# A four-layer encoder trunk on one core: the first layer's sums of squares taken from x as it is loaded, two tiles of x copied by VectorE, and a new table of order shifts

## The chip, the cores and the metric

The kernel runs on one core of one Trainium2 chip. The metric is the device time of one execution in microseconds. Three runs of the kernel before took 1061.21 to 1062.21 us, with a median of 1061.58 us.

## The reference, cut to what matters

The input x is 512 frames of 1024 channels in float32. Four layers follow each other; each is one token mixer behind an RMS norm, added to x. The mixers are differential attention (layers 0 and 3 of the program, the "first" and the "last" here), a conformer convolution (layer 1, the second) and latent attention (layer 2, the third). All are causal by chunks of 64 frames.

```python
def _rms_norm(x, g):
    xf = x.astype(jnp.float32)
    y = xf * lax.rsqrt(jnp.mean(xf * xf, axis=-1, keepdims=True) + NORM_EPS)
    return (y * g.astype(jnp.float32)).astype(x.dtype)

for i in range(DEPTH):                      # DEPTH = 4
    kind, j = i % N_MIXERS, i // N_MIXERS   # N_MIXERS = 3
    if kind == 0:
        h = _rms_norm(x, a_norm_g[j])
        x = x + _diff_attention(h, a_w_in[j], ...)   # q, k, v, gate = split(h @ w_in); 8 heads
    elif kind == 1:
        h = _rms_norm(x, b_norm_g[j])
        x = x + _conformer_conv(h, b_w_in[j], ...)   # GLU, depthwise conv of 31 taps, layer norm, gate
    else:
        h = _rms_norm(x, c_norm_g[j])
        x = x + _mla(h, c_w_in[j], ...)              # low-rank q and kv, 8 heads, gate
return x
```

What the change rewrites is the mean of x*x over the channels of each frame, for the first layer alone. What it computes stays the same.

## The kernel before, in words

Everything stays in the core's memory. `X` holds x with channels on partitions, as 8 blocks of 128 channels by 512 frames. `Hh` and `Hl` hold g*x, split into a rounded high part and the low rest. Each weight is split in the same way after its load: ScalarE casts the high half, and VectorE or GpSimd subtracts to get the low half (line 519 or 522). Each product is then three matmuls, high x high, high x low and low x high (`mm3`, line 465 for each matmul). The norm's factor 1/rms is not applied to g*x but afterwards, per frame: `rs` is 1/rms and `rs2` its square, both 128 frames by 4 tiles. The evacuation of V, the gate and the norms of q and k read them.

`start` brings x in: four tiles of 128 frames by 1024 channels, in two buffers `L0_x0` and `L0_x1` of two tiles each. TensorE transposes 4 blocks of 128x128 into one PSUM buffer `L0_tr<tile><first block>`. From it ScalarE makes four blocks of `Hh` (line 495) and one 128x512 copy into `X` (line 502), and VectorE makes four blocks of `Hl` (line 531). Then `norm_block` lets ScalarE square the 8 channel blocks of `X`, each 128x512, and GpSimd add them into `L0_sqs` (7 additions, line 522). `norm_end` sums `L0_sqs` over partitions with four matmuls against a vector of ones (`L0_ss`), VectorE scales and adds the epsilon (line 540), GpSimd raises to the power -0.5 (`L0_r_y`, line 745) and VectorE writes `rs` and `rs2`.

While this goes on, the first weights are q and k's (`L0_qk0_w0`, `_w2`, `_w4`, `_w6`, two blocks of K each). Four accumulators `L0_qk0_a0` to `_a3`, one for each tile, collect them in PSUM, and V (`L0_v0_a0` to `_a3`) and the gate (`L0_g0`) follow through the same four PSUM buffers. So V's third and fourth accumulators can begin only when VectorE and ScalarE have read those of q and k.

In the second layer the last three channel blocks are convolved on TensorE: VectorE builds the matrices `L1_wa<block>_<group>` (line 519, 128x1152), TensorE multiplies them with the shifted input `L1_u4<block>` into `L1_c<block>`, and VectorE moves the result into `V` and takes its statistics. The gate blocks `L1_g1_a0` to `_a3` are scaled into `G` by VectorE with the table `L1_tab`. VectorE also builds the third layer's rope table `L2_tab` here.

In the third layer each head has four score blocks `L2_h<head>j<block>_sc`; softmax runs on VectorE and ScalarE and leaves the weights `_p`, TensorE transposes them (`_wtr`), ScalarE copies them out (`_wt`), and TensorE multiplies them with `V` into `L2_o<head>`. The output projection of the layer, `L2_o00` to `L2_o13`, starts while the last heads still run.

All engines run their own list of instructions in order. A planner in the kernel, `Plan.order`, makes these lists before anything runs: it takes nodes one by one, with its own costs for each instruction and for each buffer's release, and among the ready ones of an engine it prefers the one with the lowest priority number. That number is the place in the program plus a shift from the table `SHIFT` (line 210), which has an entry for most sections of the program on each engine:

```python
n.prio += SHIFT.get(section(n), 0)
```

## Time and profile before

| what | value |
|---|---|
| median of three runs | 1061.58 us (1061.21 to 1062.21) |
| the profiled execution | 1064.24 us, span 1062.4 us |
| TensorE busy | 1010.8 us, 95% |
| VectorE busy | 764.4 us, 72% |
| ScalarE busy | 586.1 us, 55% |
| GpSimd busy | 216.0 us, 20% |
| bytes moved by DMA | 87.53 MB |
| clock granted to TensorE, mean | 0.987 |

The profiled execution is one run; it is 2.66 us above the median, and all durations below come from it. An engine's busy time is the time in which it executes instructions, so the 5% that TensorE lacks are gaps in its list. In the timelines a row gives the start and the length in us, the engine, the line, the operation, what it writes and reads, how many instructions the row holds, and in brackets how long the engine idled before it and which instruction ended that wait. Buffer and layer numbers are left out of the names there.

### The profile page before, as it was taken

What the parts mean: (1) busy time and instruction counts of PE and PEld (TensorE: products, weight loads), DVE (VectorE), ACT (ScalarE), POOL (GpSimd) and SP (SyncE); (2) the same over time, 40 slices, a digit from 0 to 9 for tenths busy, and PEclk for the clock granted to TensorE, in tenths of its full rate; (3) what the DMA queues carried; (4) which work ended last, traced back from release to release, by engine and by line L of the source; (5) the groups of instructions that cost most, each with busy time, mean ns of one, the idle gap of its engine ahead of it and who ended that gap; (6) DMA issues with size and microseconds to landing.
All of it is one profiled execution on the core that took longest, in us unless ns stands there. A gap on an engine that the chain in (4) does not pass through costs nothing.

```text
span 1062.4 us, 15183 instructions
## 1 busy us (share of the span) xinstructions
PE 1010.8 (95%) x5212; PEld 847.7 (80%) x5212; DVE 764.4 (72%) x1966; ACT 586.1 (55%) x1226; POOL 216.0 (20%) x142
## 2 busy tenths in 40 slices
PE   8899999998999999798999999999999999999798
PEld 6688788887887887687887778788878888887687
DVE  4767689795669998768344769964683699989651
ACT  6557266657644556653343667753443746666642
POOL 3500000000012899960530001000210000000000
PEclk9999999998999999999999999999999999999899
DMA  7252241314014332220222211112232514423102
GB/s 240 83 138 61 80 119 60 100 48 117 31 51 128 110 104 87 79 91 1 58 91 65 85 50 60 41 38 80 80 100 85 153 41 119 112 68 101 39 20 80
DMA packets 74309, 87.53 MB, mean 82 GB/s; under 512 B 17110, under 2 KB 47702, under 8 KB 74233
## 3 DMA queue, kind: packets, MB, share of 16 engines
q1 hardware_dynamic: 74232, 86.57, 27.5%
q8 instruction: 41, 0.67, 0.3%
q14 instruction: 36, 0.29, 0.1%
HBM read 75.28 MB, written 2.10 MB: 73 GB/s over the span
## 4 chain that ended last, share of the span: by engine, by line
PE 70%; POOL 8%; ACT 8%; DVE 5%; issue 4%; DMA 2%; SPq 2%; DVEq 0%; ACTq 0%; POOLq 0%
PE L_o L465 21%; PE L_qk_a L465 15%; PE L_g_a L465 10%; PE L_v_a L465 7%; PE L_ab_a L465 5%; POOL L_cq L522 4%; POOL L_sqs L522 2%; ACT G L495 1%; SPq L569 1%; PE L_c_a L465 1%; PE L_qk_tr L471 1%; PE L_h7j_sc L465 1%; PE L_h2j_sc L465 1%; PE L_h6j_sc L465 1%; DMA L_setup<-a_lam_k 1%
## 5 line engine op out<-in xcount | busy, mean ns | idle before, releaser
L465 PE MATMUL L_qk_a<-L_qk_w,Hh 128*128 128x512 f32 x512 | 163.1, 400 | 2.6 <-DVE L_qk_T L519 1.3
L465 PE MATMUL L_o<-L_y,L_o_w 128*128 128x512 f32 x576 | 143.3, 398 | 0.3 <-DVE L_y L531 0.2
L465 PEld LDWEIGHTS L_o<-L_y,L_o_w 128*128 128x128 f32 x576 | 105.7, 189 | 21.9 <-DVE L_y L519 0.9
L465 PE MATMUL L_g_a<-L_g_w,Hh 128*128 128x512 f32 x384 | 120.8, 396 | 1.2 <-DVE L_g_w L519 0.5
L745 POOL TENSOR_TENSOR L_h_or_y<-L_h_ov,minus_half 128x4 f32<-128x4 f32 x16 | 17.5, 1093 | 465.9 <-DVE L_h_ov L540 302.3
L465 PEld LDWEIGHTS L_qk_a<-L_qk_w,Hh 128*128 128x128 f32 x512 | 91.9, 189 | 19.6 <-DVE L_qk_T L519 1.5
L465 PE MATMUL L_qk_a<-L_qk_w,Hl 128*128 128x512 f32 x256 | 100.6, 393 | 2.0 <-DVE Hl L531 2.0
L522 POOL TENSOR_TENSOR L_cq<-L_cq,L_ct 128x512 f32<-128x512 f32 x58 | 84.9, 1463 | 24.7 <-ACT L_ct L495 20.7
L465 PE MATMUL L_v_a<-L_v_w,Hh 128*128 128x512 f32 x256 | 82.5, 404 | 2.1 <-DVE L_qk_T L519 2.1
L465 PEld LDWEIGHTS L_g_a<-L_g_w,Hh 128*128 128x128 f32 x384 | 70.2, 188 | 15.9 <-DVE L_g_w L519 0.9
L465 PE MATMUL L_ab_a<-Hh,L_ab_w 128*128 128x512 f32 x256 | 80.1, 391 | 0.0
L465 PE MATMUL L_g_a<-L_g_w,Hl 128*128 128x512 f32 x192 | 75.2, 391 | 0.0
L522 POOL TENSOR_TENSOR L_sqs<-L_sqs,L_sq 128x512 f32<-128x512 f32 x28 | 45.4, 1620 | 130.5 <-ACT L_sq L495 129.1
L531 DVE SCALAR_TENSOR_TENSOR L_c<-L_u,L_tab,L_c 128x512 f32<-128x512 f32 x90 | 65.6, 749 | 1.5
L519 DVE TENSOR_TENSOR L_g_w<-L_g_w_r,L_g_w 128x1024 fp32r<-128x1024 f32 x32 | 43.5, 1360 | 28.9 <-ACT L_g_w L502 28.8
L495 ACT ACTIVATE L_ct<-L_u,L_tab 128x512 f32<-128x512 f32 x60 | 43.0, 722 | 35.1 <-POOL L_cq L522 35.0
L465 PEld LDWEIGHTS L_qk_a<-L_qk_w,Hl 128*128 128x128 f32 x256 | 48.1, 188 | 13.6 <-DVE Hl L531 3.3
L502 ACT CAST L_g_w<-L_g_w_r 128x1024 fp32r<-128x1024 f32 x32 | 33.6, 1050 | 41.7 <-PE L_v_a L465 22.0
L465 PEld LDWEIGHTS L_ab_a<-Hh,L_ab_w 128*128 128x128 f32 x256 | 48.1, 188 | 10.1
L465 PEld LDWEIGHTS L_v_a<-L_v_w,Hh 128*128 128x128 f32 x256 | 46.8, 192 | 11.6 <-DVE L_qk_T L519 2.6
L502 ACT CAST L_qk_w<-L_qk_w_r 128x1024 fp32r<-128x1024 f32 (+1 forms) x33 | 33.7, 1037 | 36.3 <-PE L_o L465 14.6
L465 PE MATMUL L_v_a<-L_v_w,Hl 128*128 128x512 f32 x128 | 50.9, 398 | 0.0
(366 smaller groups left out, 2335.6 us busy)
## 6 DMA issues: line engine op xcount, KB each, us to landing
L_qk_w_r<-a_w_in SPq DMA_DIRECT2D x62, 256.0 KB, 3.0
L_v_w_r<-a_w_in SPq DMA_DIRECT2D x16, 512.0 KB, 3.8
L_g_w_r<-a_w_in SPq DMA_DIRECT2D x16, 512.0 KB, 3.7
...
```

The lines of the kernel that those rows point to most:

```text
L465: lambda nc: nc.tensor.matmul(out.real(), a.real(), b.real(), start=start, stop=stop),
L471: emit = lambda nc: nc.tensor.transpose(out.real(), src.real(), ident.real())
L495: nc.scalar.activation(out.real(), src.real(), func, scale=scale.real() if isinstance(scale, View) else scale, **kw)
L502: lambda nc: nc.scalar.copy(out.real(), src.real()), [src], [out])
L519: lambda nc: nc.vector.tensor_tensor(out=out.real(), in0=a.real(), in1=b.real(), op=op), [a, b], [out])
L522: lambda nc: nc.gpsimd.tensor_tensor(out=out.real(), in0=a.real(), in1=b.real(), op=op), [a, b], [out])
L531: self.add("dve", out.n / 960.0 + (0.13 if isinstance(scalar, View) else 0.068), lambda nc: nc.vector.scalar_tensor_tensor(out=out.real(), ...
L569: self.add("sp", 0.45, lambda nc: nc.sync.dma_start(out.real(), src.real()), [src], [out], dma=out.n * 4 * parts)
L745: self.p.add("pool", 0.32 + 0.18 * v.n, lambda nc: nc.gpsimd.tensor_tensor(out=y.real(), in0=v.real(), in1=self.minus_half[:, 0:v.n].real( ...
```

## The change

Three things are changed. First, the copies of x's tiles 2 and 3 into `X` are made by VectorE; those of tiles 0 and 1 stay on ScalarE. Second, the first layer's sums of squares are taken from the x tiles as loaded, with frames on partitions: ScalarE squares a whole tile, 128x1024, and accumulates along the row into one column of `L0_v`; the squares themselves go to `G`, which nothing reads then. VectorE scales and adds the epsilon, and a new function `norm_root` does what the end of `norm_end` did. The 8 squares of 128x512, the 7 additions on GpSimd, the four matmuls with ones and the buffer `L0_sqs` are gone from the first layer; the other layers keep them. Third, every entry of `SHIFT` is another number (920 entries before, 884 now), so the order changes in all four layers.

```diff
 SHIFT = {k: int(v) for k, v in (x.split("=") for x in """
-L0_g0_a.act=-797 L0_g0_a.pe=27679 L0_g0_w.act=699 L0_g0_w.dve=421 L0_g0_w_r.sp=4 L0_g1_a.act=686 L0_g1_a.pe=-1737
...
+L0_g0_a.act=-41 L0_g0_a.pe=26653 L0_g0_w.act=-16 L0_g0_w.dve=1363 L0_g0_w_r.sp=-471 L0_g1_a.act=2674 L0_g1_a.pe=9
...
@@ start
-                p.copy(self.X[:, k:k + 4, ts_], tr[:, :, :])
+                p.copy(self.X[:, k:k + 4, ts_], tr[:, :, :], "act" if t < 2 else "dve")
                 for q in range(4):
                     p.stt(self.Hl[:, k + q, ts_], tr[:, q, :], self.g[:, k + q:k + q + 1],
                           self.Hh[:, k + q, ts_].f32(), ALU.mult, ALU.subtract)
-        p.shift = 150
-        for k in range(NK):
-            self.norm_block(k, split=False)
-        self.norm_end()
-        p.shift = 0
+        v = self.small(4, "L0_v")
+        for t in range(NT):
+            p.act(self.G[:, t, :], tiles[t // 2][:, t % 2, :], AF.Square, accum=v[:, t:t + 1])
+        p.ts(v, v, 1.0 / D, ALU.mult, EPS, ALU.add)
+        self.norm_root(v)
@@ norm_begin
-        self.sqs = self.buf("wt", name + "_sqs", [P, S])
+        if name != "L0":
+            self.sqs = self.buf("wt", name + "_sqs", [P, S])
@@ norm_end
         v = self.small(4, N + "_v")
         p.ts(v, ps[:, :, 0], 1.0 / D, ALU.mult, EPS, ALU.add)
-        r = self.rsqrt(v, N + "_r")
+        self.norm_root(v)
+
+    def norm_root(self, v):
+        p = self.p
+        r = self.rsqrt(v, self.nname + "_r")
         p.copy(self.rs, r, "dve")
         p.tt(self.rs2, r, r, ALU.mult)
```

The lists of instructions differ in many places. Three of them follow. A row gives the line, the operation, what it writes and reads with the program's names, the shape, and how many such instructions stand together; the numbers behind the names only tell buffers apart, and all lines of the changed kernel are 5 smaller.

The first place is the start, on ScalarE and on GpSimd. ScalarE from its first instruction, before the change:

```order
L495 ACT_TABLE_LOAD
L495 ACTIVATE Hh_115<-L0_tr00_156,L0_lay_126 128x128 x4
L502 COPY X_111<-L0_tr00_156 128x4x128
L495 ACTIVATE Hh_115<-L0_tr04_162,L0_lay_126 128x128
L502 CAST L0_qk0_w0_186<-L0_qk0_w0_r_142 128x512
L495 ACTIVATE Hh_115<-L0_tr14_180,L0_lay_126 128x128 x4
L502 COPY X_111<-L0_tr14_180 128x4x128
L495 ACTIVATE Hh_115<-L0_tr10_195,L0_lay_126 128x128 x4
L502 COPY X_111<-L0_tr10_195 128x4x128
```

And with the change (`L0_lay` holds the norm's gain, `L0_qk0_w0_r` is the weight as loaded, `G`,`L0_v` are the dump and the sums of the Squares):

```order
L490 ACT_TABLE_LOAD
L490 ACTIVATE G_118,L0_v_153<-L0_x0_126 128x1024
L490 ACTIVATE Hh_115<-L0_tr04_155,L0_lay_139 128x128 x3
L497 CAST L0_qk0_w0_179<-L0_qk0_w0_r_141 128x512 x2
L490 ACTIVATE Hh_115<-L0_tr00_174,L0_lay_139 128x128 x4
L490 ACTIVATE G_118,L0_v_153<-L0_x0_126 128x1024
L490 ACTIVATE Hh_115<-L0_tr10_191,L0_lay_139 128x128 x2
L497 CAST L0_qk0_w2_213<-L0_qk0_w2_r_147 128x1024
```

A Square of the first tile now stands ahead of all blocks of `Hh`, and the second one ahead of tile 1's; the copies into `X` moved behind the casts.

GpSimd at the same place, its first work on data, with the change:

```order
L517 TENSOR_TENSOR L0_qk0_w2_213<-L0_qk0_w2_r_147,L0_qk0_w2_213 128x1024
L517 TENSOR_TENSOR L0_qk0_w4_226<-L0_qk0_w4_r_150,L0_qk0_w4_226 128x1024
L740 TENSOR_TENSOR L0_r_y_279<-L0_v_153,minus_half_114 128x4
L517 TENSOR_TENSOR L0_qk0_w6_276<-L0_qk0_w6_r_198,L0_qk0_w6_276 128x1024
L740 TENSOR_TENSOR L0_h0_or_y_916<-L0_h0_ov_911,minus_half_114 128x4
```

Before, the three low halves of `_w2`, `_w4` and `_w6` stood together, with the seven additions into `L0_sqs` and then `L0_r_y` behind them; now `L0_r_y` stands ahead of `_w6`.

The second place is VectorE in the second layer's tail, before the change:

```order
L519 TENSOR_TENSOR G_118<-L1_g1_a3_4405,L1_tab_2552 128x512
L519 TENSOR_TENSOR L1_wa5_2_4480<-L1_d4_3321,wx_112 128x1152
L519 TENSOR_TENSOR L1_wa5_3_4498<-L1_d4_3321,wx_112 128x1152
L519 TENSOR_TENSOR L1_wa6_0_4515<-L1_d4_3321,wx_112 128x1152
L519 TENSOR_TENSOR L2_tab_4521<-L2_setup_4057 128x4x64
L519 TENSOR_TENSOR L2_tab_4521<-L2_setup_4057 128x4x32
L519 TENSOR_TENSOR L1_wa6_1_4534<-L1_d4_3321,wx_112 128x1152
L519 TENSOR_TENSOR V_117<-L1_c5_4182,cb_113 128x128 x2
```

And with the change:

```order
L514 TENSOR_TENSOR G_118<-L1_g1_a2_4330,L1_tab_2528 128x512
L514 TENSOR_TENSOR L1_wa5_2_4406<-L1_d4_3297,wx_112 128x1152
L514 TENSOR_TENSOR L1_wa5_3_4425<-L1_d4_3297,wx_112 128x1152
L514 TENSOR_TENSOR L1_wa6_0_4442<-L1_d4_3297,wx_112 128x1152
L514 TENSOR_TENSOR L1_wa6_1_4454<-L1_d4_3297,wx_112 128x1152
L514 TENSOR_TENSOR V_117<-L1_c5_4085,cb_113 128x128 x4
L547 BN_STATS L1_stat_4016<-V_117 128x6 x4
L547 BN_STATS L1_stat_4016<-L1_ctr3_4449 128x6 x4
L514 TENSOR_TENSOR G_118<-L1_g1_a3_4457,L1_tab_2528 128x512
L514 TENSOR_TENSOR L2_tab_4519<-L2_setup_4026 128x4x64
```

The weight `L1_wa6_1` moved ahead of the rope table, and the last gate block, `L1_g1_a3`, behind the groups of block 5; on TensorE the four `L1_c5` groups now stand ahead of that gate block as well.

The third place is TensorE in the third layer around heads 5 and 6, before the change, from the last rows of the output projection ahead of head 5's product with `V`:

```order
L465 MATMUL L2_o03_6803<-L2_y0_6676,L2_o0_w0_6524 128x512 x6
L465 MATMUL L2_o03_6803<-L2_y1_6738,L2_o0_w2_6553 128x512 x6
L465 MATMUL L2_o01_6745<-L2_y1_6738,L2_o0_w2_6553 128x512 x6
L471 MATMUL L2_h5j0_wtr_6827<-ident_109,L2_h5j0_p_6616 128x128
L471 MATMUL L2_h5j1_wtr_6830<-ident_109,L2_h5j1_p_6637 128x128 x2
L465 MATMUL L2_h6j0_sc_6835<-L2_p3_st0_6659 128x256 x3
...
L465 MATMUL L2_o5_6853<-V_117,L2_h5j0_wt_6828 128x128
```

And with the change:

```order
L460 MATMUL L2_o00_6699<-L2_y0_6666,L2_o0_w0_6501 128x512 x3
L466 MATMUL L2_ytr3_6708<-ident_109,V_117 128x128 x4
L460 MATMUL L2_o01_6716<-L2_y0_6666,L2_o0_w0_6501 128x512 x3
L466 MATMUL L2_h5j0_wtr_6724<-ident_109,L2_h5j0_p_6577 128x128
L466 MATMUL L2_h5j1_wtr_6726<-ident_109,L2_h5j1_p_6588 128x128 x2
L460 MATMUL L2_o02_6733<-L2_y0_6666,L2_o0_w0_6501 128x512 x3
L466 MATMUL L2_p3_tr00_6741<-ident_109,L2_q3_T_6329 128x128 x4
L466 MATMUL L2_p3_tr10_6748<-ident_109,L2_q3_T_6329 128x128 x4
L460 MATMUL L2_o5_6756<-V_117,L2_h5j0_wt_6723 128x128
```

Of the output projection, 39 matmuls of 512 columns stood ahead of the first `L2_o5` row before, and 9 stand there now; head 6's scores moved behind it.

More of the change, by code (lines that the diff above doesn't have):

```diff
@@ L350 @@
-L3_v1_w.act=2427 L3_v1_w.dve=-13 L3_v1_w_r.sp=7813 L3_y0.act=-1042 L3_y1.act=4284 L3_y1.dve=-50 L3_y2.act=-30
-L3_y2.dve=-1702 L3_y3.dve=-20 L3_ytr0.pe=244 L3_ytr1.pe=-8 L3_ytr2.pe=5413 L3_ytr3.pe=1767 L3_ytr5.pe=-3471
-L3_ytr6.pe=234 L3_ytr7.pe=-11 none.act=578 none.dve=18020 none.sp=-2444
+L0_g0_a.act=-41 L0_g0_a.pe=26653 L0_g0_w.act=-16 L0_g0_w.dve=1363 L0_g0_w_r.sp=-471 L0_g1_a.act=2674 L0_g1_a.pe=9
+L0_g1_w.act=97 L0_g1_w.dve=17790 L0_g1_w_r.sp=2029 L0_h0_mx.dve=-2270 L0_h0_or_y.dve=1539 L0_h0_or_y.pool=-368
@@ new lines @@
+L1_sq3.act=-2124 L1_sq4.act=590 L1_sq5.act=-1989 L1_sq6.act=-197 L1_sq7.act=330 L1_sqs.act=1509 L1_sqs.pool=-1106
+L1_ss.pe=-9618 L1_stat.dve=1535 L1_tab.act=1801 L1_tab.dve=-152 L1_u0.dve=-2015 L1_u1.dve=1 L1_u2.dve=33073
+L1_u3.dve=-1192 L1_u45.dve=-2495 L1_u46.dve=3 L1_u46.sp=3511 L1_u47.dve=-256 L1_u47.sp=-2378 L1_v.dve=-1332
+L1_vtr.pe=2912 L1_wa5_.dve=41 L1_wa6_.dve=-1417 L1_wa7_.dve=546 L1_wxt.act=2847 L1_wxt.pe=16 L1_y0.act=250
+L1_y0.dve=5627 L1_y1.act=47 L1_y1.dve=-1188 L1_y2.act=1283 L1_y2.dve=-1229 L1_y3.act=76 L1_ytr1.pe=713
@@ new lines @@
+L2_h1_wtr.pe=-3577 L2_h2_mx.dve=-1829 L2_h2_sc.dve=380 L2_h2_sc.pe=260 L2_h2_wt.act=1436 L2_h2_wtr.pe=12579
+L2_h3_mx.dve=-1997 L2_h3_p.act=191 L2_h3_sc.dve=686 L2_h3_sc.pe=17196 L2_h3_wt.act=-241 L2_h3_wtr.pe=23947
+L2_h4_mx.dve=1 L2_h4_p.act=-1571 L2_h4_sc.dve=23559 L2_h4_sc.pe=87 L2_h4_wt.act=-1816 L2_h4_wtr.pe=1211
+L2_h5_mx.dve=-944 L2_h5_p.act=-15 L2_h5_sc.dve=1911 L2_h5_sc.pe=1205 L2_h5_wt.act=18 L2_h5_wtr.pe=1331
+L2_h6_mx.dve=1029 L2_h6_p.act=-161 L2_h6_sc.dve=-4071 L2_h6_sc.pe=-681 L2_h6_wt.act=1169 L2_h6_wtr.pe=-5297
@@ new lines @@
+L3_h1_oss.dve=-462 L3_h1_ov.dve=6 L3_h1_p.act=4811 L3_h1_p.dve=97 L3_h1_sc.dve=22663 L3_h1_sc.pe=-2103
+L3_h1_wt.act=316 L3_h1_wtr.pe=-1575 L3_h2_cf.dve=-19071 L3_h2_mx.dve=-2004 L3_h2_or_y.dve=529 L3_h2_or_y.pool=2572
+L3_h2_osq.act=-2776 L3_h2_oss.dve=-1251 L3_h2_ov.dve=-208 L3_h2_p.act=-5058 L3_h2_p.dve=38 L3_h2_sc.dve=2398
+L3_h2_sc.pe=-7821 L3_h2_wt.act=14301 L3_h2_wtr.pe=-3318 L3_h3_cf.dve=32 L3_h3_mx.dve=563 L3_h3_or_y.dve=2098
+L3_h3_or_y.pool=-116 L3_h3_osq.act=5652 L3_h3_oss.dve=-139 L3_h3_ov.dve=337 L3_h3_p.act=-370 L3_h3_p.dve=-148
@@ new lines @@
+L3_o12.pe=-7163 L3_o130.pe=-1724 L3_o131.pe=84245 L3_o1_w.act=-10417 L3_o1_w.dve=-459 L3_o1_w_r.sp=1930
+L3_o2.dve=-9008 L3_o2.pe=-3288 L3_o3.dve=2429 L3_o3.pe=-848 L3_o4.dve=-1820 L3_o4.pe=-1577 L3_o5.pe=-1710
+L3_o6.dve=1005 L3_o6.pe=-44 L3_o7.dve=-97 L3_o7.pe=-5 L3_ot000.act=-1631 L3_ot000.sp=-474 L3_ot010.sp=8
+L3_ot020.act=1104 L3_ot020.sp=1041 L3_ot030.act=-2656 L3_ot030.sp=2301 L3_ot100.act=1693 L3_ot100.sp=122
+L3_ot110.act=610 L3_ot110.sp=-420 L3_ot120.act=-2179 L3_ot120.sp=-216 L3_ot130.act=20621 L3_ot130.sp=-439
@@ new lines @@
+L3_ot13256.sp=30 L3_qk0_T.dve=577 L3_qk0_a.pe=-477 L3_qk0_ss.dve=43410 L3_qk0_st.act=-385 L3_qk0_st.dve=-1022
+L3_qk0_st.sp=1201 L3_qk0_t.dve=-19 L3_qk0_tr.pe=15880 L3_qk0_w.act=1952 L3_qk0_w.dve=4596 L3_qk0_w_r.sp=-578
+L3_qk0_y.dve=-1432 L3_qk1_T.dve=-66 L3_qk1_a.pe=47647 L3_qk1_ss.dve=171 L3_qk1_st.act=1192 L3_qk1_st.dve=-9004
+L3_qk1_st.sp=4764 L3_qk1_t.dve=-229 L3_qk1_tr.pe=-2412 L3_qk1_v.dve=22 L3_qk1_w.act=-133 L3_qk1_w.dve=976
+L3_qk1_w_r.sp=-13540 L3_qk1_y.dve=-985 L3_qk2_T.dve=-4 L3_qk2_a.pe=246 L3_qk2_sq.act=3743 L3_qk2_ss.dve=69611
@@ new lines @@
+L3_sq4.act=245 L3_sq5.act=-272 L3_sq6.act=-425 L3_sq7.act=32 L3_sqs.act=2425 L3_sqs.pool=-2404 L3_tab.dve=15
+L3_v.dve=2050 L3_v0_a.act=2798 L3_v0_a.pe=1620 L3_v0_w.act=721 L3_v0_w.dve=705 L3_v0_w_r.sp=-556 L3_v1_a.act=3413
+L3_v1_a.pe=1 L3_v1_w.act=1026 L3_v1_w.dve=5611 L3_v1_w_r.sp=1964 L3_y0.act=-14 L3_y0.dve=181 L3_y1.act=1615
+L3_y1.dve=5 L3_y2.act=303 L3_y3.act=227 L3_ytr0.pe=-146 L3_ytr1.pe=5627 L3_ytr2.pe=10596 L3_ytr3.pe=54
+L3_ytr4.pe=-1549 L3_ytr5.pe=-15504 L3_ytr7.pe=1143 none.dve=22412 none.sp=-7301
```

243 lines of the change are left out of this document (105 added, 138 removed).

## The prediction

> **What bounds the kernel now.** I read the page first, then the chain of waits, TensorE's waits by cause, and the timelines of the places where the order differs.
>
> ```profile
> span 1062.4 us, 15183 instructions
> PE 1010.8 (95%) x5212; PEld 847.7 (80%) x5212; DVE 764.4 (72%) x1966; ACT 586.1 (55%) x1226; POOL 216.0 (20%) x142
> PE 70%; POOL 8%; ACT 8%; DVE 5%; issue 4%; DMA 2%; SPq 2%; DVEq 0%; ACTq 0%; POOLq 0%
> ```
>
> ```profile
> 52.09 13.28 PE L_v_a L465 x51
> ...
> 859.86 5.48 PE L_qk_a L465 x24
> ```
>
> TensorE is busy for 1010.8 of 1062.4 us, and the change takes almost no matmul away: only its 51.6 us without work, and stretches in which it works below full speed, can be gained. The two last rows are pieces of the chain (start, length, what): V's product ends at 65.37, and the second is my unit, since 24 matmuls of 512 columns in 5.48 us are 0.228 us each, and a three-product group is 0.68 us. The waits, summed by cause, show where the idle time lies (us in total, times, the longest):
>
> ```profile
> PE L_o L465 <- DVE V L531: 6.6, 2, 3.6
> PE L_ytr L471 <- DVE V L540: 4.7, 1, 4.7
> PE L_g_a L465 <- DVE G L519: 4.4, 3, 3.0
> ...
> PE L_ss L465 <- POOL L_sqs L522: 1.7, 3, 1.0
> ```
>
> They are many and small, these four 17.4 us together, and most hang on VectorE. Only the last one, in the first of its three places, belongs to what the change rewrites by hand; the rest can move only through the new order.
>
> **The start: what is removed.** The first layer's rms statistics are made from X, the copy behind the transposes, so they come late (the timeline; in brackets how long the engine idled before, and for whom):
>
> ```profile
> 35.66 3.63 POOL L522 TENSOR_TENSOR L_sqs<-L_sqs,L_sq 128x512 f32<-128x512 f32 x1 [11.90 <-ACT L_sq L495]
> 41.97 9.01 POOL L522 TENSOR_TENSOR L_sqs<-L_sqs,L_sq 128x512 f32<-128x512 f32 x5 [0.65 <-ACT L_sq L495]
> 47.01 0.72 PE L465 MATMUL L_v_a<-L_v_w,Hh 128*128 128x512 f32 x2 [2.14 <-DVE L_qk_T L519]
> ...
> 51.03 1.05 PE L465 MATMUL L_ss<-ones,L_sqs 128*128 128x1 f32 x8 [0.96 <-POOL L_sqs L522]
> 51.95 0.84 PE L465 MATMUL L_v_a<-L_v_w,Hh 128*128 128x512 f32 x2
> ...
> 55.58 0.71 PE L465 MATMUL L_v_a<-L_v_w,Hh 128*128 128x512 f32 x2
> ```
>
> TensorE first waits 2.14 us for two accumulators that VectorE empties, then 0.96 us for GpSimd's last addition, then sums over partitions from 51.03 to 51.95, which is 0.92 us. From 51.95 to 55.58 nine matmuls take 3.63 us, 0.40 each instead of 0.228: 9 x 0.228 = 2.05, so 1.58 us are lost after the two waits. The window row of these 20 us shows the clock at 0.91:
>
> ```profile
> 40.00:60.00 20.00, 16.90 (x71) 13.25 (x70) 15.60 (x33) 6.59 (x10) 11.93 (x7) 0.91 0.35 104
> ```
>
> [...] If these waits were not its cause, the 1.58 us would stay and the sum below would lead to 1058.0; I go by the row, in which nothing else stands ahead of the slow matmuls.
>
> With the sums gone, 0.96 + 0.92 + 1.58 = 3.46 us go. The 2.14 us shrink as well, because VectorE and GpSimd hold each other up:
>
> ```profile
> 36.33 0.68 DVE L519 TENSOR_TENSOR L_qk_T<-L_qk_T,L_qk_t 128x512 f32<-128x512 f32 x1
> 42.33 1.79 DVE L519 TENSOR_TENSOR L_qk_T<-L_qk_T,L_qk_t 128x512 f32<-128x512 f32 x1
> ```
>
> At 36.33 the addition takes 0.68 us, and it is GpSimd's addition beside it that is long (3.63 us, against 9.01 for the next five). At 42.33, beside those five, the same addition takes 1.79: 1.11 more, ahead of the evacuation that TensorE waits for. I take 1.11; the bounds are 0 (what else stands before the accumulators of tiles 2 and 3 fills the gap: in the new order VectorE has four X copies and the second half of its rope products there) and 2.14 (the wait goes). Removed: 3.46 + 1.11 = **4.57 us**.
>
> **The start: what is added.** The timeline again, with the nearest rows to each new instruction:
>
> ```profile
> 19.86 1.05 ACT L502 CAST L_qk_w<-L_qk_w_r 128x1024 fp32r<-128x1024 f32 x1 [0.36 <-DMA L_qk_w_r<-a_w_in]
> 956.12 0.20 ACT L495 ACTIVATION_READ_ACCUMULATOR L_h5j_p<-L_h5j_sc,L_h5j_mx,L_rq 128x1 f32 x1
> 21.57 0.59 ACT L502 COPY X<-L_tr 128x512 f32<-128x512 f32 x1
> 33.48 0.63 ACT L495 ACTIVATE L_sqs<-X 128x512 f32<-128x512 f32 x1
> 29.18 1.44 DVE L519 TENSOR_TENSOR L_qk_t<-L_qk_a,L_tab 128x256 f32<-128x256 f32 x4 [6.11 <-ACT L_qk_sq L495]
> 20.98 2.78 POOL L522 TENSOR_TENSOR L_qk_w<-L_qk_w_r,L_qk_w 128x1024 fp32r<-128x1024 f32 x1 [3.23 <-ACT L_qk_w L502]
> 37.23 0.62 PE L465 MATMUL L_v_a<-L_v_w,Hh 128*128 128x512 f32 x2
> 52.37 1.95 POOL L745 TENSOR_TENSOR L_r_y<-L_v,minus_half 128x4 f32<-128x4 f32 x1 [1.38 <-DVE L_v L540]
> ```
>
> No row is a Square of 1024 elements. A 1024-element cast on the same engine is 1.05 us and reading an accumulator 0.20: **1.25 us** each, an estimate from these rows. Four make 5.0 us, as much as the eight old Squares (8 x 0.63 = 5.04), and four X copies (2.36) leave ScalarE. What counts is the place: the old ones begin at 33.48, and the new ones stand in the first 20 us, between the Hh blocks and weight casts that TensorE waits for. The first stands ahead of every Hh block, so I charge one in full, 1.25 us. The others stand where TensorE has groups at hand: tiles 0 and 1 now run over all of K first, 16 groups of 0.68 = 10.9 us, before tiles 2 and 3 begin. Bounds: 0 (the first Square fits into the wait for g and the weights) and 5.0 (none is covered).
>
> GpSimd's r_y now stands between the second and the last low half of the first weights. It is 1.95 us, so with nothing else changed the last low half ends at 20.98 + 2.78 + 1.95 = 25.7. Behind it 20 groups remain, 13.7 us, and one set of transposes, 0.5 as an estimate, so V would begin at 39.9, which is 2.7 later than 37.23: 1.5 more than the 1.25 charged. Against this, that weight's load now moves ahead of the setup loads on SP's queue. If the 3.23 us that GpSimd idles before it go with that, the low half ends at 22.5 and V begins at 36.7, 0.5 early. I keep the 1.25, which lies between these ends.
>
> The four X copies on VectorE have no row; its nearest PSUM operation of that size is a share of the 0.68 us row, so 2.7 us for four, against 0 if only the copied bytes counted. They lie in the 6.11 us that VectorE idles before 29.18. If the setup loads come late, they fall behind its wait for these, and the Hl blocks after them are late; that cost is within the 5.0. Start in sum: 4.57 - 1.25 = **3.32 us** gained.
>
> **The second layer's tail.** VectorE builds the next layer's rope table and a convolution weight in an order that TensorE waits for:
>
> ```profile
> 466.40 3.24 DVE L519 TENSOR_TENSOR L_tab<-L_setup 128x256 f32<-128x256 f32 x2
> 469.56 1.34 DVE L519 TENSOR_TENSOR L_wa<-L_d,wx 128x1152 f32<-128x1152 f32 x1
> 470.96 11.95 PE L465 MATMUL L_c<-L_wa,L_u 128*128 128x128 f32 x90 [1.85 <-DVE L_wa L519]
> ```
>
> 3.24 us of table stand ahead of the weight, and TensorE idles 1.85. In the new order four weights stand ahead of the table: the 1.85 go. What is late next is the gate block that now follows the convolution groups; bounds 0 and 1.85.
>
> Sum: 3.32 + 1.85 = 5.2 us. The profiled execution took 1064.24 us (its span and 1.84 around it), 2.66 above the median of the runs, 1061.58. From 1064.24 the sum leads to 1059.0; on the runs' scale **1056.4 us**. The rest of the new order I take as 0 with no view to price it: it touches rows of TensorE in all four layers, so I allow a quarter of the 17.4 us of waits above, 4 us, both ways.
>
> **Rivals.**
>
> *The lead is lost again: no change.* Further on VectorE is nearly full:
>
> ```profile
> 220.00:240.00 20.00, 20.00 (x98) 16.68 (x97) 19.47 (x49) 11.92 (x18) 0.00 (x0) 1.00 0.14 46
> ```
>
> VectorE (the third busy column) is busy 19.47 of 20 us. If it sets the pace of the first attention, TensorE arrives 3.32 us earlier and waits longer there. Against it: TensorE is busy for all 20.00 in the same row, so both are full and VectorE gains the lead too. Only the 1.85 would stay, and less if the gate block takes it: 1059.7 to 1061.6, say 1060.5. Chance 0.20.
>
> *A larger gain.* The gate blocks of the second layer are TensorE's other series of waits:
>
> ```profile
> 404.07 0.47 PE L465 MATMUL L_g_a<-Hh,L_g_w 128*128 128x512 f32 x1 [1.36 <-DVE L_ab_v L519]
> 432.50 0.47 PE L465 MATMUL L_g_a<-Hh,L_g_w 128*128 128x512 f32 x1 [3.00 <-DVE G L519]
> 439.99 0.50 PE L465 MATMUL L_g_a<-Hh,L_g_w 128*128 128x512 f32 x1 [1.65 <-DVE L_u L558]
> 446.80 0.50 PE L465 MATMUL L_g_a<-Hh,L_g_w 128*128 128x512 f32 x1 [1.05 <-DVE G L519]
> ```
>
> The new order puts the last gate block behind convolution groups. If all four go, 1.36 + 3.00 + 1.65 + 1.05 = 7.06 us more: 1056.4 - 7.1 = 1049.3. For it: the groups now ahead of the last block are free of G. Against it: the first three blocks keep VectorE's scaling ahead of them. Chance 0.16.
>
> *Slower: the third layer's heads lose their cover.* Before the first product of head 5's weights with V, TensorE now has 39 output-projection matmuls; in the new order 9 stand there. The first row here is 18 of the 39; the second is from the last layer, where heads run without such cover:
>
> ```profile
> 703.25 4.37 PE L465 MATMUL L_o<-L_y,L_o_w 128*128 128x512 f32 x18
> 986.48 0.94 PE L465 MATMUL L_o<-V,L_h5j_wt 128*128 128x128 f32 x6 [3.55 <-DVE V L531]
> ```
>
> The 30 that leave are 30 x 0.228 = 6.8 us. If softmax on VectorE and ScalarE is not ready, that much idling appears at head 5, of which the last layer shows 3.55 us in one wait. Added to the forecast, 6.8 gives 1063.2; with a slow stretch like the 1.58 behind it and the 1.5 of the late last weight it reaches 1066.3. It decides from 7.3 us of new idling on, since 5.2 + 2.1 must be used up. Against it: the 30 matmuls cover the later heads instead, and the page's waits show no idling at head 5 now, so there is some slack. Chance 0.17.
>
> **How the numbers follow.** Forecast 0.47, no change 0.20, larger gain 0.16, slower 0.17. The forecast's own range is 1052 to 1059.4: the unpriced 4 us down, and up to where it would be no change. This kernel's measurement can tell 0.2%, 2.1 us, from nothing. Faster is the forecast and the larger gain, 0.63; within 0.2% the first rival, 0.20; slower 0.17. The range over the cases is 1047.5 to 1064: it holds most of the larger gain and the near end of the slower one.
>
> **What would show it.** Right: no wait on the sums, no slow stretch behind 51 us and no 1.79 us row in the first 60 us, V ending 3 us or so earlier than 65.37; a table behind the weights at about 466 us and no 1.85. Wrong: the first 512-column matmul or the last weight of the first four more than 2 us late; TensorE's idling before 65 us unchanged; new waits at head 5 of the third layer of 5 us or more; or a lead at 65 us that is gone at the end of the first layer.

## The result, and the profile after

The changed kernel takes 1050.20 us (median of four runs, 1048.62 to 1052.12), against 1061.89 (1061.21 to 1062.44) for the kernel before beside it. The paired comparison gives a ratio of 0.9872, with a 95% interval of 0.9841 to 0.9904. By the medians 11.7 us are gained, where 5.2 were forecast: inside the range, but below the likeliest case's own 1052 to 1059.4. Two runs in the groups below lie far off, one of kernel 6 (4823.24 us) and one of the kernel before beside kernel 10 (1682.52 us), and the ratios leave them out.

The head of the page of the kernel after:

```profile
span 1050.3 us, 15191 instructions
PE 1006.6 (96%) x5204; PEld 848.2 (81%) x5204; DVE 769.3 (73%) x1970; ACT 586.2 (56%) x1222; POOL 197.5 (19%) x135
```

The busy time of TensorE fell by 4.2 us (with 8 matmuls fewer: the profile counts two for each of the four sums), and the span by 12.1; so about two thirds are gaps in TensorE's work that closed. Where, is seen when both executions are cut at the same events: the first V product, the second q/k chunk's first product, the first product of the second, third and fourth layer, the end. The columns are the stretch and its length, the busy time of TensorE, its weight loads, VectorE, ScalarE and GpSimd (with counts), TensorE's granted clock, the DMA share and GB/s. Before:

```profile
0.00:37.23 37.23, 32.46 (x156) 25.83 (x157) 19.70 (x61) 23.35 (x55) 9.87 (x10) 1.00 0.55 174
37.23:97.96 60.73, 57.63 (x283) 47.68 (x282) 43.94 (x119) 33.77 (x74) 15.01 (x9) 0.97 0.39 113
97.96:305.73 207.77, 201.51 (x1047) 168.94 (x1045) 158.55 (x475) 122.51 (x276) 7.42 (x7) 0.98 0.26 75
305.73:542.47 236.74, 220.16 (x1084) 183.70 (x1082) 184.96 (x279) 119.81 (x171) 144.62 (x89) 0.99 0.27 80
542.47:759.22 216.75, 208.31 (x1155) 179.37 (x1154) 147.47 (x435) 125.52 (x300) 24.72 (x17) 0.99 0.21 63
759.22:1062.30 303.08, 290.69 (x1495) 242.19 (x1493) 209.73 (x601) 161.16 (x353) 14.36 (x11) 0.99 0.29 86
```

And after:

```profile
0.00:37.57 37.57, 32.87 (x156) 27.01 (x157) 25.32 (x67) 25.04 (x57) 8.81 (x10) 1.00 0.60 189
37.57:92.08 54.51, 54.51 (x275) 45.92 (x273) 41.52 (x124) 31.83 (x71) 1.02 (x1) 1.00 0.39 114
92.08:299.30 207.22, 200.51 (x1046) 167.44 (x1045) 158.13 (x467) 120.89 (x273) 7.07 (x7) 0.99 0.27 75
299.30:536.98 237.68, 222.06 (x1083) 184.50 (x1082) 187.11 (x278) 120.94 (x171) 145.26 (x89) 0.97 0.27 80
536.98:748.66 211.68, 205.99 (x1156) 178.82 (x1155) 147.69 (x436) 126.35 (x300) 22.61 (x17) 1.00 0.22 65
748.66:1050.20 301.54, 290.68 (x1495) 244.50 (x1493) 209.56 (x601) 161.20 (x353) 12.74 (x11) 0.98 0.29 86
```

Row by row, the gains are -0.34, 6.22, 0.55, -0.94, 5.07 and 1.54 us: 12.1 in all. Two rows hold it: the first V stretch, which the prediction priced, and the third layer, which it took as nothing. In the second row of after, TensorE is busy for all 54.51 us at a clock of 1.00, where it idled 3.10 us and ran at 0.97 before.

A row also holds the stretches in which TensorE works at about half speed (before, the granted clock from 51.95 to 55.58 is 0.56), and these do not fall in the same places in every profile. Over the whole execution the mean granted clock is 0.987 in both profiles: what the first V stretch and the third layer gained in clock, the second layer (0.97 against 0.99) and the last (0.98 against 0.99) lost. The gaps alone, length less busy time, shrank by 3.10 us in the second row, 0.96 in the second layer, 2.75 in the third and 1.53 in the last, and grew by 0.45 in the third row.

The timeline of the start, after (TensorE, then ScalarE, VectorE, GpSimd):

```profile
37.57 0.61 PE L460 MATMUL L_v_a<-L_v_w,Hh 128*128 128x512 f32 x2
60.93 0.39 PE L460 MATMUL L_v_a<-L_v_w,Hl 128*128 128x512 f32 x1
...
4.32 1.06 ACT L490 ACTIVATE G<-L_x 128x1024 f32<-128x1024 f32 x1 [2.30 <-DMA L_x<-x]
5.28 0.19 ACT L490 ACTIVATION_READ_ACCUMULATOR G<-L_x 128x1 f32 x1
...
18.73 2.59 DVE L514 TENSOR_TENSOR L_tab<-L_setup 128x256 f32<-128x256 f32 x1
22.67 0.42 DVE L514 TENSOR_TENSOR L_tab<-L_setup 128x256 f32<-128x256 f32 x1
35.65 0.69 DVE L514 TENSOR_TENSOR L_qk_T<-L_qk_T,L_qk_t 128x512 f32<-128x512 f32 x1
...
17.23 1.02 POOL L740 TENSOR_TENSOR L_r_y<-L_v,minus_half 128x4 f32<-128x4 f32 x1 [0.57 <-DVE L_v L535]
18.67 2.37 POOL L517 TENSOR_TENSOR L_qk_w<-L_qk_w_r,L_qk_w 128x1024 fp32r<-128x1024 f32 x1 [0.42 <-ACT L_qk_w L497]
```

V begins at 37.57 and ends at 60.93 + 0.39 = 61.32, 4.05 us earlier than the 65.37 of before, and no row in between has a wait: neither the 0.96 for the sums nor the 2.14 for the accumulators is left. The Square and its reading cost 1.06 + 0.19 = 1.25 us, as estimated. The first one begins when its x has landed, while TensorE transposes the same x; the first block of `Hh` begins at 5.73 behind it, against 5.95 before. The last low half ends at 18.67 + 2.37 = 21.04.

The second layer's gate blocks and its tail, after:

```profile
398.32 0.47 PE L460 MATMUL L_g_a<-Hh,L_g_w 128*128 128x512 f32 x1 [0.85 <-DVE L_ab_v L514]
407.22 0.50 PE L460 MATMUL L_g_a<-Hh,L_g_w 128*128 128x512 f32 x1 [2.29 <-DVE G L514]
427.87 0.76 PE L460 MATMUL L_g_a<-Hh,L_g_w 128*128 128x512 f32 x1 [2.95 <-ACT L_ct L490]
437.13 0.50 PE L460 MATMUL L_g_a<-Hh,L_g_w 128*128 128x512 f32 x1 [0.78 <-DVE G L514]
471.58 8.66 PE L460 MATMUL L_c<-L_wa,L_u 128*128 128x128 f32 x74 [2.11 <-DVE L_wa L514]
...
466.76 3.50 DVE L514 TENSOR_TENSOR L_tab<-L_setup 128x128 f32<-128x128 f32 x2
470.18 1.34 DVE L514 TENSOR_TENSOR L_wa<-L_d,wx 128x1152 f32<-128x1152 f32 x1
...
460.50 9.61 POOL L517 TENSOR_TENSOR L_o_w<-L_o_w_r,L_o_w 128x1024 fp32r<-128x1024 f32 x4 [5.64 <-ACT L_o_w L497]
```

The gate blocks still wait 0.85 + 2.29 + 2.95 + 0.78 = 6.87 us (7.06 before), and the 1.85 has become 2.11, some matmuls later. All its gaps together are 15.62 us, against 16.58 before; the row is 0.94 us longer because TensorE's busy time grew by 1.90 at the lower clock. So the second layer won at most the 0.96 us of gaps, and the time does not show it.

The third layer, where the unpriced gain is. First two places of before, the key and value products of a pair of heads (`L_kv_a`) and head 4:

```profile
597.35 0.96 PE L465 MATMUL L_kv_a<-L_kv_w,L_lat 128*128 128x512 f32 x3 [1.55 <-ACT V L502]
...
682.26 0.33 PE L471 MATMUL L_h4j_wtr<-ident,L_h4j_p 128*128 128x128 f32 x1 [1.06 <-ACT L_h4j_p L495]
683.35 0.49 PE L465 MATMUL L_o<-V,L_h4j_wt 128*128 128x128 f32 x2 [0.77 <-ACT L_h4j_wt L502]
683.60 1.43 PE L465 MATMUL L_h4j_sc<-L_p_st 128*128 128x512 f32 x3
```

After, the 1.55 is gone, and head 4 has:

```profile
672.44 0.33 PE L466 MATMUL L_h4j_wtr<-ident,L_h4j_p 128*128 128x128 f32 x1 [0.35 <-ACT L_h4j_p L490]
683.66 0.94 PE L460 MATMUL L_h5j_sc<-L_p_st 128*128 128x512 f32 x3
```

Three score matmuls of 512 columns took 1.43 us before, behind the two waits (head 4's); the same form takes 0.94 after at nearly the same time (head 5's); the granted clock over these rows is 0.58 and 1.00. So a second slow stretch is gone here. The waits around it are not fewer: after, heads 4 and 5 show five between 672 and 682 us, 0.29 to 0.61 us each and 2.35 in sum, but none is as long as the 1.06. That the slow stretch went because of this is not shown. The longest wait for head 5 itself is 0.50 us.

### The profile page after: what moved, and what is told of

Same layout as the page of the kernel before. It is cut to its first block, busy times and chain, and to the rows that moved or that the text cites. A ratio compares the mean times of both kernels' runs of the same rounds, so it can differ in the third digit from the quotient of the medians.

```text
span 1050.3 us, 15191 instructions
## 1 busy us (share of the span) xinstructions
PE 1006.6 (96%) x5204; PEld 848.2 (81%) x5204; DVE 769.3 (73%) x1970; ACT 586.2 (56%) x1222; POOL 197.5 (19%) x135
## 4 chain that ended last, share of the span: by engine, by line
PE 73%; DVE 10%; POOL 6%; ACT 5%; issue 4%; ACTq 0%; POOLq 0%; DVEq 0%
PE L_o L460 21%; PE L_qk_a L460 15%; PE L_g_a L460 11%; PE L_v_a L460 8%; POOL L_cq L517 4%; PE L_ab_a L460 3%; DVE L_c L526 2%; PE L_c_a L460 2%; PE L_ytr L466 1%; ACT G L490 1%; PE L_qk_tr L466 1%; PE L_h7j_sc L460 1%; POOL L_sqs L517 1%; PE L_h3j_sc L460 1%; PE L_h6j_sc L460 1%
## 5 line engine op out<-in xcount | busy, mean ns | idle before, releaser
L460 PE MATMUL L_o<-L_y,L_o_w 128*128 128x512 f32 x576 | 139.8, 394 | 0.0
L497 ACT CAST L_qk_st<-L_qk_tr 64x512 fp32r<-64x512 f32 x64 | 37.0, 581 | 29.5 <-PE L_qk_tr L466 28.6
L517 POOL TENSOR_TENSOR L_sqs<-L_sqs,L_sq 128x512 f32<-128x512 f32 x21 | 31.3, 1490 | 113.7 <-ACT L_sq L490 61.9
L514 DVE TENSOR_TENSOR L_qk_w<-L_qk_w_r,L_qk_w 128x1024 fp32r<-128x1024 f32 (+1 forms) x30 | 35.3, 1186 | 23.5 <-ACT L_qk_w L497 23.3
```

The costliest lines, as they stand in the source:

```text
L460: lambda nc: nc.tensor.matmul(out.real(), a.real(), b.real(), start=start, stop=stop),
L497: lambda nc: nc.scalar.copy(out.real(), src.real()), [src], [out])
L514: lambda nc: nc.vector.tensor_tensor(out=out.real(), in0=a.real(), in1=b.real(), op=op), [a, b], [out])
L517: lambda nc: nc.gpsimd.tensor_tensor(out=out.real(), in0=a.real(), in1=b.real(), op=op), [a, b], [out])
```

## The experiments

Each kernel below holds the first-layer code of before or after and has its four engines' lists written out, so that only the named rows move; "old" and "new" mean the lists of before and after. Where a list with rows from the other could not be run in that order, a few instructions stand one to six places off. The kernels have other line numbers (a matmul is L609). The V stage is the stretch from the first V product to the first gate product. Times are medians; each ratio is against the kernel before on the same chip, whose medians were 1061.82, 1063.46, 1064.08 and 1063.41 in the four groups (1059.5 to 1069.6 over the 25 runs of the first), so the ratios are compared, and the stages by the profiles.

**1. The arithmetic alone, in the old order.** Lists of before; copies on ScalarE; the eight old Squares, seven additions and four sums are left out.

```diff
 ScalarE, old list
+Square x tile 0
 Hh of tile 0 ...
+Square x tile 1
 Hh of tile 1 (second half of K) ...
 cast of the weight w4
+Square x tiles 2, 3
```

> The kernel before with every engine's list as it was, except that the first layer's statistics come from four Squares on x as loaded (the first ahead of all other work of ScalarE, the second ahead of the second tile's high parts, the third and fourth behind the cast of the third weight); the 8 squares, 7 additions and 4 matmuls with ones are gone, and X is still copied by ScalarE. Theory A (the arithmetic change pays by itself): the wait for the sums (0.96 us), the sums (0.92) and the slow stretch (1.58) go and the 2.14 us wait shrinks by about 1.1, less the Squares' place: V ends 3 to 5 us earlier than 65.37 and the total is 3 to 5 us less. Theory B (the new order is what pays): V's wait for its accumulators stays or grows, the Squares delay the first products, V ends within 1.5 us of before and the total is the same.

Measured: 1060.96 us, ratio 0.9979 (0.9960 to 0.9998). Start and V stage (windows), and two TensorE rows ahead of V:

```profile
0.00:41.52 41.52, 32.93 (x157) 25.86 (x157) 21.87 (x61) 26.63 (x61) 8.10 (x9) 1.00 0.50 156
41.52:64.51 22.99, 22.99 (x109) 19.19 (x108) 15.28 (x36) 7.85 (x10) 1.02 (x1) 1.00 0.52 160
```

```profile
17.44 0.72 PE L609 MATMUL L_qk_a<-L_qk_w,Hh 128*128 128x512 f32 x2 [1.47 <-ACT Hh L639]
26.13 0.50 PE L609 MATMUL L_qk_a<-L_qk_w,Hl 128*128 128x512 f32 x1 [1.46 <-DVE Hl L675]
```

V begins 4.29 us later than before, and TensorE idles 41.52 - 32.93 = 8.59 us ahead of it (4.77 before): the Squares hold up `Hh`, and through it `Hl`. Behind that, V runs without a wait at clock 1.00 and pays it back. So the arithmetic alone is worth 0.9 us by the medians, 2.2 by the ratio; either is less than the 3 to 5 us of theory A. The cost of the Squares in a bad place is near the bound of 5.0; in the new order it is the 0.34 of the first row above.

**2. GpSimd's additions put back, with nothing waiting for them.** Kernel 1, and seven additions of `X` into a buffer that nobody reads:

```diff
 GpSimd, list of kernel 1
+7 x TENSOR_TENSOR dummy <- dummy, X  128x512
 r_y
```

> As the run with the Squares, with seven additions of 128x512 put back on GpSimd where they stood, on blocks of X, into a buffer that nothing reads and nothing waits for. Theory A (the two engines hold each other up): VectorE's additions beside them take about 1.8 us instead of 0.7, and 1 to 2 us of the wait for V's accumulators come back against the run without them; the slow stretch of the clock may come back with it. Theory B (GpSimd's work beside VectorE costs nothing by itself): the same as the run without them, within 0.3 us at V's end.

Measured: 1066.05 us, ratio 1.0031 (1.0013 to 1.0049): 5.1 us above kernel 1. The V stage, and rows of GpSimd, VectorE and TensorE:

```profile
41.36:69.45 28.09, 25.30 (x109) 20.12 (x108) 20.24 (x38) 7.84 (x10) 9.78 (x6) 0.94 0.44 131
```

```profile
39.04 11.39 POOL L666 TENSOR_TENSOR L_dmy<-L_dmy,X 128x512 f32<-128x512 f32 x6
54.07 1.02 POOL L917 TENSOR_TENSOR L_r_y<-L_v,minus_half 128x4 f32<-128x4 f32 x1 [3.64 <-DVE L_v L684]
...
41.34 1.78 DVE L663 TENSOR_TENSOR L_qk_T<-L_qk_T,L_qk_t 128x512 f32<-128x512 f32 x1
...
52.17 0.94 PE L609 MATMUL L_v_a<-L_v_w,Hh 128*128 128x512 f32 x2 [1.89 <-DVE L_qk_T L663]
53.33 1.05 PE L609 MATMUL L_v_a<-L_v_w,Hh 128*128 128x512 f32 x2
```

The stage is 28.09 us instead of 22.99, 5.10 more for the same 109 matmuls. Between 39 and 52 us the same six instructions of VectorE, four subtractions for V's weights and two additions, take 11.31 us where kernel 1 took 6.27, so 5.04 more (the busy time of the window, 20.24 against 15.28, counts two instructions more). The 1.78 us addition is back, TensorE waits 0.90 us for one of the subtractions and 1.89 us for a write of `L_qk_T`, and behind that the three products from 52.17 to 53.33 (one row of the group is left out here) take 0.39 us each instead of 0.228 (the granted clock from 52.17 to 55.89 is 0.55). Nothing waits for these additions, and `L0_r_y`, which stands behind them on GpSimd, begins 3.64 us after the last of them, released by VectorE; so what they cost, they cost through VectorE. It is more than the 1 to 2 us that theory A gave. The same addition takes 1.78 us beside GpSimd's seven and 0.69 in kernel 1, which has none of them.

**3. Two of the Squares later.** Kernel 1 with the Squares of tiles 2 and 3 behind tile 3's first copy; those of tiles 0 and 1 cannot go so late, since the setup loads reuse tile 0's buffer.

```diff
 ScalarE, list of kernel 1
-Square x tiles 2, 3      (behind the cast of w4)
 ...
 copy X of tile 3 (second half of K)
+Square x tiles 2, 3
```

> As the run with the Squares in the old order, with the third and the fourth Square moved to ScalarE's gap behind the first copy of the last tile. There V began 4.3 us late. Theory A (each Square in the old order costs its own length, 1.25 us, where high parts and casts wait behind it): V begins 2.5 us earlier than in that run, at about 39, and since V's accumulators are then needed earlier some of the wait for them returns, at most 2.1 us. Theory B (the first two hold up everything, by the load of the setup behind them): V begins where it did, within 0.5 us.

Measured: 1060.27 us, ratio 0.9946 (0.9922 to 0.9971). In this profile the first 512-column product begins at 11.00, 1.53 us later than in kernel 1: x landed 0.28 us later, and the transposes and the matmuls on ones (`L_warm`) behind it took longer, for which the profile shows no cause. Counted from that product, V begins after 30.15 us, against 32.05 in kernel 1, 27.98 before and 28.10 after. So 1.9 of the 4.1 us are these two Squares' place, nearer to the 2.5 of theory A than to the 0.5 of theory B.

**4. New first layer, old rest.** The kernel after, with every row that is not of the first layer in the old order.

```diff
 every engine, new list
-rows of L1, L2, L3 in the new order
+the same rows in the old order, in the same places
```

> The changed kernel in its first layer, code and lists, with the lists of the other three layers as they were before. Theory A (each layer's gain is its own): the lead is 5.5 to 6.5 us at the second layer's first product, stays there to the end, and the total is about 6 us less than before. Theory B (the lead at the start is given back or grows by what follows from it): 2 us or less, or 10 us or more at the end.

Measured: 1058.38 us, ratio 0.9956 (0.9930 to 0.9982). The second layer, and the third up to head 1's first score and from there on:

```profile
298.98:534.36 235.38, 220.02 (x1084) 182.98 (x1082) 184.49 (x279) 119.95 (x171) 144.39 (x89) 0.99 0.28 81
534.36:626.29 91.93, 86.89 (x425) 73.48 (x424) 51.45 (x155) 48.85 (x111) 12.35 (x9) 1.00 0.27 79
626.29:751.70 125.41, 121.69 (x732) 106.30 (x731) 95.96 (x281) 76.68 (x189) 12.37 (x8) 0.99 0.16 51
```

In the profile the lead is 6.75 us at the second layer's first product. The new first layer alone is worth 3.4 us by the medians and 4.7 by the ratio (the profiled execution, 1055.73 us, is at the short end of its ten), so the times do not show that all of the lead lasts. The third layer is entered 8.1 us earlier than before and still takes 91.93 + 125.41 = 217.34 us (216.75 before): its gain does not come from being entered earlier.

**5. The copies on ScalarE, everything else as after.**

```diff
-copy X of tiles 2, 3 on VectorE
+copy X of tiles 2, 3 on ScalarE, behind each tile's Hh
```

> The changed kernel with the four copies of tiles 2 and 3 back on ScalarE, each behind its tile's high parts, and all else in the changed order. Theory A (the copies lie beside other work on either engine, as the prediction took them): V begins within 0.5 us of 37.57 and the total is the same. Theory B (VectorE's copies relieve ScalarE, which holds up the high parts): V begins 1 us later or more, up to the 2.4 us of four copies.

Measured: 1051.79 us, ratio 0.9880 (0.9841 to 0.9919), which overlaps the kernel after's. V begins at 37.51 (37.57 after). The copies' engine is worth nothing that these runs can tell, up to 1.6 us by the medians.

**6. The new order of the last two layers alone, and its reverse.**

```diff
 first kernel:  code of before; lists old, rows of L2 and L3 new
 second kernel: code of after;  lists new, rows of L2 and L3 old
```

> The kernel before with the third and the fourth layer's instructions in the changed kernel's order; the transplant of the third alone lost 9.5 us around its end, where its list and the fourth layer's loads and weight casts are woven together. Theory A (the gain lies in these lists once they are whole): the third layer takes 211 to 213 us, the fourth 301 to 302, and the total is 5 to 7 us less than before. Theory B (it came from the earlier start or the clock): the third layer takes 216 us or more, the total within 1.5 us of before.

> The changed kernel with the third and the fourth layer's instructions in the order of before. Theory A: the lead of 5 to 6 us at the third layer's start is kept but doesn't grow, so the total is 5 to 7 us less than before and 5 to 7 us more than the changed kernel. Theory B: the lead grows by 5 us in the third layer as in the changed kernel.

Measured: 1067.82 us, ratio 1.0025 (0.9999 to 1.0052), and 1062.09 us, ratio 0.9989 (0.9969 to 1.0009). The third layer took 218.97 and 220.98 us: longer than 216.75 in both, and longest up to head 1, as the second kernel's window shows:

```profile
536.81:631.72 94.91, 88.39 (x425) 74.57 (x424) 51.99 (x156) 49.13 (x111) 12.31 (x9) 0.98 0.26 78
```

And the first kernel's two windows, with the same cut:

```profile
547.61:642.99 95.38, 88.29 (x424) 74.40 (x423) 55.04 (x159) 49.45 (x112) 10.65 (x9) 0.98 0.27 77
642.99:766.58 123.59, 119.92 (x733) 105.20 (x732) 96.11 (x281) 77.61 (x189) 11.93 (x8) 1.00 0.16 51
```

Whichever half is exchanged, the third layer loses some 3 us up to head 1 against the kernel before, where the two orders meet. Away from that border, from head 1 on, it goes by its own list: 123.59 us with the new rows, 126.07 with the old ones (122.93 after, 124.89 before). Theory A falls for both: the first kernel's third layer is longer, and the second has nothing left of its lead at the end.

**7. The third layer's new order in the kernel before, whole and in one piece.**

```diff
 first kernel:  code of before; lists old, rows of L2 new
 second kernel: code of before; lists old, rows of L2's first q and kv chunk, its gate, latent and their transposes new
```

> The kernel before with the third layer's instructions in the changed kernel's order and nothing else changed. Theory A (the third layer's gain lies in its own lists): the third layer takes about 212 us instead of 217, and the total is about 5 us less. Theory B (it came from the earlier start, or from where the clock's slow stretches happened to fall): the third layer takes 216 us or more and the total is the same within 1.5 us.

> The kernel before with one inner piece of the third layer in the changed kernel's order: the first pair of heads' q and kv products with their evacuation, the latent's transposes and the second gate block; both ends of the layer are as before. From the layer's first product to head 1's first score it took 91.8 to 92.8 us in five profiles with the whole old order, 88.5 to 88.8 with the whole new one, and 94.9 to 95.4 in three transplants that cut at the layer's end. Theory A (the gain lies in this list; the transplants lost it at the cut): 1.5 to 3 us less, 89 to 90.3, with the 1.55 us wait for V's copy gone. Theory B (the gain isn't in this list): 91.5 or more.

Measured: 1077.56 us, ratio 1.0128 (1.0092 to 1.0164), and 1074.49 us, ratio 1.0098 (1.0066 to 1.0131). The third layer took 226.25 and 228.25 us; up to head 1's first score the second took 104.18, where theory A gave 89 to 90.3. The second kernel's waits there:

```profile
588.74 0.45 PE L609 MATMUL L_q_a<-L_q_w,L_lat 128*128 128x384 f32 x1 [2.66 <-ACT L_q_w L646]
611.34 1.77 PE L615 MATMUL L_p_tr<-ident,L_q_T 128*128 128x128 f32 x8 [3.09 <-DVE L_q_T L663]
```

The moved rows of TensorE now wait for weight casts and rope products whose engines' neighbouring rows kept the other order. The theory that the third layer's list is good by itself falls with this; a piece of it costs time. From head 1 on the first of the two took 131.13 us, where kernel 6 took 123.59 with the fourth layer's rows new as well: by these two profiles that part of the third layer does badly without the fourth's rows beside its own.

**8. The second layer's inner rows old, the rest as after.**

```diff
 every engine, new list
-L1's a/b, u, convolution, gate, weight, table rows in the new order
+the same rows in the old order, in the same places
```

> The changed kernel with the inner part of the second layer (input products, convolution, gates, the matrices for TensorE; not the norm ahead of it nor the output projection) in the order of before. In the profiles so far the second layer took 235.4 to 236.7 us in the old order and 237.7 in the new one. Theory A (the new order of this layer is a loss by itself): the second layer takes 1 to 2 us less than 237.7, and so does the total. Theory B (the difference came from what is woven in at its ends): 237 us or more, the total the same.

Measured: 1049.78 us, ratio 0.9865 (0.9826 to 0.9905). The second layer took 235.05 us instead of 237.68, and the third still 211.63.

```profile
299.51:534.56 235.05, 219.78 (x1084) 182.91 (x1082) 182.98 (x278) 119.97 (x171) 144.55 (x89) 0.99 0.27 81
```

Of the 2.63 us, 222.06 - 219.78 = 2.28 are busy time of TensorE, at a clock of 0.99 instead of 0.97; the gaps are 15.27 us instead of 15.62. So this profile holds fewer slow stretches, and neither it nor the times show that the new order of the second layer is a loss.

**9. The rope table behind the copies and `Hl` of tiles 2 and 3, in the first layer.**

```diff
 VectorE, new list
-products of the rope table and setup
 X copies and Hl of tiles 2, 3
+products of the rope table and setup
```

> The changed kernel with one thing moved: in VectorE's list at the start the products of the rope table stand behind the copies and low parts of tiles 2 and 3 instead of ahead of them. In the changed kernel the first of these products took 2.59 us beside GpSimd's subtraction for the fourth weight, and TensorE waited 1.38 us for the low part behind it. Theory A (that product was held by GpSimd, and the wait is on the path): the 1.38 us wait goes and V begins 0.8 to 1.4 us earlier than 37.57. Theory B (another wait stands right behind it, such as that for the fourth weight's low half, ready at 21.04): V begins within 0.4 us of 37.57.

Of the four blocks of tiles 2 and 3, three stand ahead of the products then; the last one keeps its place behind them.

Measured: 1049.80 us, ratio 0.9861 (0.9815 to 0.9906), no different from after. The three products that took 2.59 + 0.28 + 0.28 us now take 0.82 together. The 128x4 product that stands beside GpSimd's subtraction in their place (it makes `rs2`) takes 1.44 us instead of 0.15, and both end within 0.02 us of each other. V begins at 36.30, 1.27 us earlier than after, but then:

```profile
41.29 0.70 PE L609 MATMUL L_v_a<-L_v_w,Hh 128*128 128x512 f32 x2 [0.75 <-DVE L_qk_T L663]
```

The lead is down to 0.28 us at the first gate product and gone by the second V chunk: a wait for VectorE's accumulators takes it back. This is the mechanism of the rival that forecast no change, seen on a smaller gain.

**10. Both of the last two.** The edits of 8 and 9 together.

> The changed kernel with both edits that came out well in the profiles: the rope table's products moved behind the copies and low parts at the start, and the inner part of the second layer in the order of before. Theory A (what the second layer gained in the profile, 2.6 us, is its own and holds): that layer takes about 235 us, the third and fourth as in the changed kernel, and the total is 1047 to 1049.5 us. Theory B (slow stretches of the clock fall elsewhere and take it back): the total is 1049.5 to 1051 us, as for the changed kernel.

Measured: 1048.52 us, ratio 0.9866 (0.9845 to 0.9886), the lowest median here; its interval lies over that of after, so it is not shown to be faster. The second layer took 236.16 us at a clock of 0.97, not the 235 of theory A.

## Why the prediction was right or wrong

**The sign and the range were right, the size was not.** Of 12.1 us between the profiles, 6 lie where the prediction put 3.3, 5 where it put 0, and its 1.85 did not come.

**Removed at the start: 4.57, measured 5.60.** The 0.96 wait, the 0.92 of sums and the 1.58 of slow matmuls went, as said. Kernels 1 and 2 show that in the V stage the slow stretch hangs on the waits: without waits there is none (clock 1.00), and with the additions it is back behind a 1.89 us wait (0.55). In the whole execution the 1.58 cannot be seen, since the mean clock is the same before and after.

The mis-sized term is the third one: "I take 1.11" of the 2.14 us wait, and the whole 2.14 went. The 1.11 counted one lengthened addition. The prediction did not see that the accumulators of before were late by another way as well (ScalarE, then VectorE):

```profile
39.33 0.63 ACT L495 ACTIVATE L_sq<-X 128x512 f32<-128x512 f32 x1 [1.84 <-POOL L_sqs L522]
39.87 0.58 ACT L495 ACTIVATE L_qk_sq<-L_qk_a 128x512 f32<-128x512 f32 x1
...
40.48 0.69 DVE L545 TENSOR_REDUCE L_qk_ss<-L_qk_sq 128x8 f32<-128x512 f32 x1 [2.33 <-ACT L_qk_sq L495]
```

GpSimd's first addition ends at 35.66 + 3.63 = 39.29. ScalarE's next Square waits 1.84 us for it, the square of q and k stands behind that Square, and VectorE idles 2.33 us for this one, ahead of all that it still has to do before the accumulators are free. Behind it, two subtractions beside the additions take 1.33 and 1.64 us, where kernel 1 has 1.22 and 1.23. In kernel 2 ScalarE waits for no addition, so that kernel shows the way through VectorE's own instructions alone. Of the 6.22 us in the second window 0.6 is not assigned.

**Added at the start: 1.25, measured 0.34.** The sum of the Square's price was exact, but the place was better than charged: the first Square runs while TensorE transposes its x, and the first block of `Hh` is not later for it. The 0.34 is the net of all that moved ahead of V. The upper bound of 5.0 was no idle fear, since the old order pays 4.29 for the same four Squares. For w6's low half both ends were too late: it ended at 21.04, not 22.5 to 25.7. `L0_r_y` took 1.02 us there and not the 1.95 that it took before, when a subtraction of VectorE (1.23 us from 52.20 on) ran beside it, and the weight came earlier. The copies at 0 stand (kernel 5).

**The second layer's tail: 1.85, measured -0.26.** The step that failed is "four weights stand ahead of the table: the 1.85 go". The weight that waited did move ahead; but the table then stands ahead of another one of the same series, `L1_wa6_3`, and TensorE waits 2.11 for that. The rows I had looked at ended before it. "What is late next is the gate block" was wrong as well. The table is long in both kernels: after, two products take 3.50 us and end at 470.26, where GpSimd's four low halves end at 460.50 + 9.61 = 470.11; before, they take 3.24 and end at 469.64, where GpSimd's last low half ends at 469.48. By kernels 2 and 9 the overlap with GpSimd is the likely price, and moving the table past a weight leaves it where it is; no run moved the low halves here, so this is argued only.

**The rest of the order: 0, measured 5.07 in the third layer, 1.54 behind it and 0.55 in the rest of the first, less 0.94 in the second.** This step failed most: "a quarter of the 17.4 us of waits" was a width without a view behind it. The third layer is short with the complete new lists and long with the old ones, with no overlap. Up to head 1's first score and from there on, old lists gave 91.76 to 92.77 and 124.75 to 125.41 us in five profiles (before and kernels 1 to 4), new lists 88.52 to 88.75 and 122.85 to 123.13 in five (after and kernels 5, 8, 9, 10). Up to head 1 it is gaps: TensorE idles 4.9 to 5.1 us there with the old lists and 2.4 with the new ones, in all ten. From head 1 on it is mostly the slow stretch: four of the five old profiles have a clock of 0.99 and gaps of 3.4 to 3.7 us, kernel 1 has 1.00 and 4.87 us, and the five new ones 1.00 and 3.3 to 3.4. For this part kernels 6 and 7 speak for the new rows of the third and fourth layer together (123.59) and against the third's alone (131.13), with one profile each; kernel 7's second kernel took 124.07 there with old rows. For the part up to head 1, 3.1 us, which rows bring it stays open: every transplant lost at its border what there was to see.

**The rivals.** *No change* was wrong: in kernel 4 the lead of the first layer is not lost in the profile, and 3.4 to 4.7 us of it are in the times. Kernel 9 shows that the mechanism is real where TensorE alone is made earlier. *The larger gain* came near in time, 1049.3, and not in cause: the four gate waits are 6.87 instead of 7.06. *Slower through head 5* did not happen: the longest wait for it is 0.50 us, so the 6.8 us of cover could be spared.
